# Log-sum-exp over head rows: the middle stage of the tile schedule removed, the half-unit stage begun three tiles earlier

## The chip, the cores and the metric

The kernel runs on one core of a Trainium2 chip. The metric is the device time of one execution in microseconds (us). The text says PE for TensorE, ACT for ScalarE, DVE for VectorE, POOL for GpSimd and SP for SyncE, as the profile does.

## The reference

`x` is 8 x 2048 x 2048 fp32, `bias` is 8 heads x 256 fp32. Each row of 2048 is split into 8 heads of 256 columns; the bias of the head is added, and the log of the sum of the exponentials is taken over the 256 columns. Each result is written twice.

```python
x_heads = x.reshape(B, S, H, Dh).transpose(0, 2, 1, 3) + bias[None, :, None, :]
x_tiled = np.repeat(x_heads, 2, axis=2)
mx = x_tiled.max(axis=-1, keepdims=True)
out = mx.squeeze(-1) + np.log(np.exp(x_tiled - mx).sum(axis=-1))      # 8 x 8 x 4096
```

## The kernel before, in words

The input is read as 64 tiles `t` = 0 to 63 of 256 rows: 128 partitions with `K` = 2 rows each, 2 MB a tile. The kernel sums plain exponentials without subtracting the maximum; a check at the end would redo everything if a sum had run out of range, and does not take place with this data.

Eight tile buffers (`xts`, pairs of them are the four buffers `xb`) hold tiles in turn, so tile `t + 8` is loaded into the buffer of tile `t` once all that read or wrote there have finished. These are gathered in `last_uses[t]`, and `reload(t)` puts the load of tile `t + 8` on SP's queue. Tiles 2 to 41 are loaded in pairs; later ones one at a time, and where a tile is worked in halves (one row of each partition, a "half unit", written 57k0 and 57k1 below) each half has its own load (`load`, `pieces`). A load also waits until the eighth load before it has landed, since there are eight completion semaphores.

There are three ways to the bias. PE can put the bias into PSUM (`put_bias`), add `x` to it with a product with the identity (`add_x`, or `late_heads` in the bulk), and ACT then takes exp from PSUM with its sum at once. POOL can add the bias to `x` in place (`g_add`). Or ACT takes exp of the bare `x`, and exp(bias) is multiplied in later: by a DVE instruction that multiplies and sums one head of one row (`weigh`), or by POOL, which multiplies and halves the columns three times down to 32 (`fold`), after which DVE sums the 32 (`add_fold`).

`STAGES` says which tile is worked how:

- bulk, tiles 0 to 53: PE takes heads 0 to 2, POOL adds the bias of heads 4 to 7, head 3 is multiplied by exp(bias) on DVE (the `mul` in `later`, L430), and one DVE reduction (L437) sums heads 1 to 7.
- mixed, tiles 54 to 56, whole tiles: PE takes head 0, POOL adds the bias of heads 4 to 7 (L412), DVE weighs heads 1 to 3 of both rows (six `weigh`, L453) and one reduction (L437) sums heads 4 to 7.
- half units from tile 57: PE takes heads 0 and 1, one ACT instruction takes exp of the other six (L418), DVE weighs heads 2 to 6, POOL folds head 7. Tiles 62 and 63 vary the shares a little, and tile 63 is loaded in eight pieces.

The order on every engine is the order of the program text, written out by hand: a loop over tiles and their pieces, with two lists of postponed work. `for_pool` holds what follows POOL's step (`later`, `add_fold`, `reload`) and `for_pe` holds ACT's reading of the PSUM sums (`sum_biased`, L393); both are flushed within the next unit, `for_pool` ahead of the unit's own exp, `for_pe` behind it. `keep_warm` puts three dummy products on PE in half units. exp(bias) of heads 1 and 2 is made once in PSUM (`first_factors`: a product that spreads the bias over the partitions, L235, then an ACT exp, L268), in the bank that the bulk uses for head 0. Two tiles after the last one of each of the eight batches, the sums of that batch are transposed on PE (L497) and ACT takes the log (L507). After tile 63 the same is done for the last batch (L606, L612) and the result is stored (L613).

Of the kernel before, what the change touches and what calls it, by code (L numbers as in the profile page):

```python
# [17 lines left out]
K = 2  # L18
# [2 lines left out]

NBUF = 8

NEARLY = 5

NWARM = 3
# [5 lines left out]


BULK = dict(pe=3, acc=1, g0=4, late=True, fold=0)
MIXED = dict(pe=1, acc=1, g0=4, late=False, fold=0)
PROMPT_F1 = dict(pe=2, acc=2, g0=8, late=False, fold=1)
PROMPT_F2 = dict(pe=2, acc=2, g0=8, late=False, fold=2)
SINGLE_F1 = dict(pe=1, acc=1, g0=8, late=False, fold=1)
# [8 lines left out]

STAGES = [
    (0, (BULK,)),
    (54, (MIXED,)),  # L50
    (57, (PROMPT_F1, PROMPT_F1)),
    (62, (SINGLE_F1, SINGLE_F1)),
    (63, (PROMPT_F2, TRIPLE)),
]
# [8 lines left out]
def kernel(  # L63
# [6 lines left out]
    nc = tc.nc  # L70
    P = nc.NUM_PARTITIONS
    B, S, D = x.shape
    H, Dh = bias.shape
# [4 lines left out]
    T = B * NBLK  # L78
    T_PROMPT = STAGES[1][0]
# [36 lines left out]
    xts = [xb[:, k : k + K] for xb in xbs for k in range(0, KB, K)]  # L116
# [8 lines left out]
    def modes_of(t):  # L125
        return [modes for t0, modes in STAGES if t0 <= t][-1]

    def pieces(t):

        if len(modes_of(t)) == 1:  # L130
            return [(0, K, 0, D)]
        cols = [[(0, D)]] * K if t < T - 1 else LAST_COLS
        return [(k, k + 1, c0, c1) for k in range(K) for c0, c1 in cols[k]]

    def rows_of(t, n=1):


        b, at = divmod(t, NBLK)
        if b < B - 1:
            blk, i = divmod(at, TB)  # L140
            v = x[b, blk * P * KB : (blk + 1) * P * KB, :]
            return v.rearrange("(p k) d -> p k d", k=KB)[:, i * K : (i + n) * K]
        v = x[b, at * P * K : (at + 1) * P * K, :]
        return v.rearrange("(k p) d -> p k d", k=K)
# [5 lines left out]
    def on_x(t, ins, after):  # L150
        buf = users[t // TB % len(xbs)]
        for t_u, u in buf:
            same = u.ins.engine == ins.ins.engine
            if u not in after and (not same or t_u % NBUF == t % NBUF and t_u < t):
                tc.declare_no_dep(
                    ins.ins,
                    u.ins,
                    reason="another tile, or waited for by those it waits for",
                )
        buf.append((t, ins))  # L160
        return ins

    loads = {}

    last_uses = [[] for _ in range(T)]

    def load(t):
        if TB <= t < BLOCKS:

            if t % TB == 0:  # L170
                after = [u for i in range(TB) if t >= NBUF for u in last_uses[t + i - NBUF]]
                ins = on_x(
                    t,
                    nc.sync.dma_start(
                        out=xbs[t // TB % len(xbs)], in_=rows_of(t, TB)
                    ),
                    after,
                )
                for i in range(TB):
                    loads[t + i, 0, 0] = ins  # L180
            return
        after = last_uses[t - NBUF] if t >= NBUF else []
        for k0, k1, c0, c1 in pieces(t):
            loads[t, k0, c0] = on_x(
                t,
                nc.sync.dma_start(
                    out=xts[t % NBUF][:, k0:k1, c0:c1],
                    in_=rows_of(t)[:, k0:k1, c0:c1],
                ),
                after,  # L190
            )

    def reload(t):

        n = t + NBUF
        if n < BLOCKS:
            if n % TB == TB - 1:
                load(n - TB + 1)
        elif n < T:
            load(n)  # L200
# [15 lines left out]
    for t in range(NBUF):  # L216
        load(t)
# [16 lines left out]
    def spread(dst, c0, c1):  # L234
        nc.tensor.matmul(  # L235
            dst, lhsT=ones, rhs=brow[:, c0:c1], start=True, stop=True
        )

    for i, c in enumerate(range(G0, D, MM)):
# [11 lines left out]
        out=b_far,  # L251
        in_=brow,
# [5 lines left out]
        out=Rx[0][0:1, 1 + NR :],  # L258
# [7 lines left out]
    def first_factors():  # L266
        spread(one_ps, V0, W0)
        nc.scalar.activation(out=one_ps, in_=one_ps, func=ACT.Exp)  # L268

    def other_factors():  # L270
        nc.scalar.activation(
            out=w_ps[:, W_LATE - W0 :], in_=b_rep[:, W_LATE - G0 : W2 - G0], func=ACT.Exp
        )
        nc.scalar.activation(out=w_sb, in_=b_rep[:, W1 - G0 :], func=ACT.Exp)
# [14 lines left out]
    def put_bias(m, k0, k1):  # L289
# [3 lines left out]
        if m["late"]:  # L293
# [4 lines left out]
            parts = [(ones3, b3)]  # L298
            if n_ps[0] <= NEARLY:
                parts = [(ones3[0:1], bparts[:, i]) for i in range(3)]  # L300
# [164 lines left out]
    def fold(t, k, h0, h1, sums, after):  # L465


        v = xts[t % NBUF][:, k, h0 * Dh : h1 * Dh]
        done = nc.gpsimd.tensor_tensor(  # L469
            out=v, in0=v, in1=w_sb[:, h0 * Dh - W1 : h1 * Dh - W1], op=ALU.mult  # L470
        )
        on_x(t, done, [after])
        v = v.rearrange("p (h j) -> p h j", j=Dh)
        n = Dh
        while n > FOLD:
            n //= 2
            done = nc.gpsimd.tensor_tensor(  # L477
                out=v[:, :, 0:n], in0=v[:, :, 0:n], in1=v[:, :, n : 2 * n], op=ALU.add
            )
            on_x(t, done, [])  # L480

        def add_fold():
            red = nc.vector.tensor_reduce(
                out=sums[:, k, h0:h1],
                in_=v[:, :, 0:FOLD],
                op=ALU.add,
                axis=mybir.AxisListType.X,
            )
            on_x(t, red, [done])

        return add_fold

# [126 lines left out]
    def sums_of(t):  # L619

        b, blk = divmod(t, NBLK)
        if b < B - 1:
            return R[b][:, blk % TB * K :, :, blk // TB]
        return R_last[:, :, blk, :].rearrange("p h k -> p k h")
# [4 lines left out]
    for_pe = []  # L629
# [15 lines left out]
    for t in range(T):  # L645
        if t == T_FACTORS:
            other_factors()
        xt = xts[t % NBUF]
        sums = sums_of(t)
        for k0, k1, c0, c1 in pieces(t):  # L650
            m = modes_of(t)[k0]
            add = None
            heads = []
            if c0 == 0:
                bias_here = bias_there
            if m["late"]:
                pe_part = late_heads(m, t, bias_here, sums)
            else:
                heads = add_x(m, t, k0, c0, c1, bias_here)

                def pe_part(t=t, heads=heads, sums=sums):
                    for k, h, bank, p, mm in heads:
                        sum_biased(t, k, h, bank, p, mm, sums)

            if c0 == 0:
                if next_units and not m["late"]:
                    bias_there = put_bias(*next_units.pop(0))
                if t > T_PROMPT and m["g0"] == H:
                    keep_warm()
                if m["g0"] < H:  # L670
                    add = g_add(m, t, k0, k1)
                if t < T - 1 or k0 == 0:
                    flush(for_pool)
            if t == T_PROMPT and (k0, c0) == (0, 0):
                first_factors()
            h0 = max(c0 // Dh, m["pe"])
            h1 = min(c1 // Dh, m["g0"])
            hf = max(h0, min(h1, H - m["fold"]))
            if h0 < h1 and not m["late"]:
                done = exp_inplace(  # L680
                    t, xt[:, k0:k1, h0 * Dh : h1 * Dh], loads[t, k0, c0]
                )
                if hf < h1:
                    for_pool.append(fold(t, k0, hf, h1, sums, done))
            if c0 == 0:
                flush(for_pe)
            if not m["late"]:
                for k in range(k0, k1):
                    for h in range(h0, hf):
                        weigh(  # L690
                            t,
                            xt[:, k, h * Dh : (h + 1) * Dh],
                            h,
                            sums[:, k, h : h + 1],
                            done,
                        )

            def pool_part(t=t, m=m, k0=k0, k1=k1, sums=sums, add=add):
                if add:
                    later(m, t, k0, k1, sums, add)  # L700
                if k1 == K:
                    reload(t)

            for_pool.append(pool_part)
            if m["g0"] < H:
                pe_part()
                if m["late"]:
                    bias_there = put_bias(*next_units.pop(0))
            elif heads:
                for_pe.append(pe_part)  # L710

        fb, at = divmod(t - 2, NBLK)
        if fb >= 0 and at == NBLK - 1:
            finish(fb)
            ends_of(fb)
            if fb == B - 2:
                store()
# [39 lines left out]
```

## Time and profile before

| | before |
|---|---|
| median of 3 runs (lowest, highest) | 326.43 us (326.16, 326.53) |
| profiled execution, its own time | 327.41 us |
| its span | 325.5 us |
| busy: DVE, POOL, PE, ACT | 289.4, 287.5, 272.7, 265.6 us |
| HBM read, written | 134.23 MB, 1.05 MB |
| mean DMA rate over the span | 416 GB/s |
| granted PE clock, mean | 0.909 |

The span runs from the first to the last instruction of the profiled execution; its own time is 1.9 us more, which lies around the span. Times in the text are us from the start of the span. A busy share is an average over the whole run, and the stages differ; what bounds the end has to be read from the last 60 us.

### The profile page before, as it was taken

The numbers are of one execution on the slowest core, as the hardware profiler recorded it, in microseconds if no ns is written. First come the engines' busy times: TensorE is split into PE (matmuls) and PEld (weight loads), VectorE is DVE, ScalarE is ACT, GpSimd is POOL, SyncE is SP. The second block draws the span as 40 slices with busy tenths as digits, with TensorE's granted clock in tenths as the row PEclk, the third lists the DMA queues.
The fourth block names the chain that finished last, engine by engine and source line by source line (L and its number), as shares of the span: only waits on it lengthen the run. The fifth ranks groups of instructions, "written<-read, shape, count | busy, mean of one in ns | idle before, by whom it ended". The sixth has DMA issues, their size and how long they took to land.

```text
span 325.5 us, 2458 instructions
## 1 busy us (share of the span) xinstructions
PE 272.7 (84%) x695; PEld 102.8 (32%) x695; DVE 289.4 (89%) x329; ACT 265.6 (82%) x426; POOL 287.5 (88%) x120
## 2 busy tenths in 40 slices
PE   5999999878898869888688878698999786598983
PEld 2333333322233323332233323233333232135451
DVE  1346879999999998989989999969999999999996
ACT  1157789898598987889889979869899699989993
POOL 6939997999999899999999999999999999858872
PEclk9977899999597997979899979778999799589999
DMA  8999999999999999999999999999999999999992
GB/s 307 464 403 439 451 417 420 447 439 407 443 443 408 437 435 431 423 439 432 419 443 434 415 443 431 407 433 427 427 421 430 429 424 424 417 421 415 421 391 93
DMA packets 8832, 135.44 MB, mean 416 GB/s; under 512 B 1041, under 2 KB 1425, under 8 KB 2417
## 3 DMA queue, kind: packets, MB, share of 16 engines
q1 hardware_dynamic: 8720, 135.27, 98.0%
q8 instruction: 5, 0.08, 0.1%
q14 instruction: 9, 0.07, 0.1%
q10 hardware_dynamic: 98, 0.01, 0.0%
HBM read 134.23 MB, written 1.05 MB: 416 GB/s over the span
## 4 chain that ended last, share of the span: by engine, by line
DVE 43%; DMA 26%; PE 18%; ACT 8%; POOL 3%; issue 0%; SPq 0%; DVEq 0%
DVE R L437 28%; DMA xb<-in_x_dram 26%; DVE xb L453 9%; PE pair L362 7%; ACT xb L418 6%; DVE xb L430 4%; PE one_ps L362 4%; POOL xb L412 3%; PE pair L303 3%; PE one_ps L303 2%; PE pair L235 1%; ACT xb L380 1%; ACT xb L373 1%; DMA brow<-in_bias_dram 1%; ACT res L507 1%
## 5 line engine op out<-in xcount | busy, mean ns | idle before, releaser
L412 POOL TENSOR_TENSOR xb<-xb,b_rep 128x2048 f32<-128x2048 f32 x57 | 257.3, 4537 | 21.3 <-DMA xb<-in_x_dram 21.1
L437 DVE TENSOR_REDUCE R<-xb 128x14 f32<-128x3584 f32 (+1 forms) x57 | 216.8, 3804 | 1.9
L418 ACT ACTIVATE xb<-xb 128x2560 f32<-128x2560 f32 (+5 forms) x77 | 157.5, 2055 | 8.2 <-POOL xb L412 8.0
L362 PE MATMUL pair<-xb,ident 128*128 128x512 f32 x216 | 117.3, 671 | 0.0
L362 PE MATMUL one_ps<-xb,ident 128*128 128x512 f32 x108 | 68.1, 716 | 10.9 <-DMA xb<-in_x_dram 10.9
L380 ACT ACTIVATE xb<-pair 128x1024 f32<-128x1024 f32 x54 | 56.0, 1038 | 25.0 <-PE pair L362 25.0
L362 PEld LDWEIGHTS pair<-xb,ident 128*128 128x128 f32 x216 | 47.0, 218 | 62.6 <-issue 62.6
L430 DVE TENSOR_TENSOR xb<-xb,w_ps 128x512 f32<-128x512 f32 x54 | 36.8, 681 | 24.0 <-ACT xb L418 23.9
L373 ACT ACTIVATE xb<-one_ps 128x256 f32<-128x256 f32 x108 | 40.4, 387 | 6.7 <-PE one_ps L362 6.7
L303 PEld LDWEIGHTS <-ones 3*128 3x128 bf16 (+1 forms) x192 | 16.8, 95 | 78.0 <-issue 69.0
L303 PE MATMUL one_ps<-b,ones 3*128 3x512 bf16 x49 | 19.1, 390 | 20.9 <-ACT xb L373 20.9
L303 PE MATMUL pair<-b,ones 3*128 3x512 bf16 x98 | 29.1, 376 | 0.0
L362 PEld LDWEIGHTS one_ps<-xb,ident 128*128 128x128 f32 x108 | 17.2, 201 | 33.7 <-DMA xb<-in_x_dram 17.3
L338 PE MATMUL pair<-xb,ident 128*128 128x512 f32 (+1 forms) x36 | 20.5, 656 | 6.3 <-DMA xb<-in_x_dram 6.3
L373 ACT ACTIVATION_READ_ACCUMULATOR xb<-one_ps 128x1 f32 x108 | 23.0, 213 | 0.0
L453 DVE CUSTOM_DVE_ANT_0 xb<-xb,w_ps 128x256 f32<-128x256 f32 x61 | 22.3, 416 | 0.0
L477 POOL TENSOR_TENSOR xb<-xb 128x128 f32<-128x128 f32 (+3 forms) x39 | 13.9, 357 | 3.1
L469 POOL TENSOR_TENSOR xb<-xb,w_sb 128x256 f32<-128x256 f32 (+1 forms) x13 | 10.0, 772 | 5.2 <-ACT xb L418 4.6
L353 PE MATMUL tp<-ident 128*128 128x128 f32 x84 | 13.0, 291 | 0.9 <-ACT res L507 0.9
L507 ACT ACTIVATE res<-tp 32x1024 f32<-32x1024 f32 x7 | 7.1, 1011 | 6.2 <-PE tp L497 6.2
L393 ACT ACTIVATE xb<-pair 128x256 f32<-128x256 f32 x33 | 12.0, 368 | 0.0
L353 PEld LDWEIGHTS tp<-ident 128*128 128x128 f32 x84 | 10.5, 191 | 4.3 <-issue 2.8
(55 smaller groups left out, 91.8 us busy)
## 6 DMA issues: line engine op xcount, KB each, us to landing
xb<-in_x_dram SPq DMA_DIRECT2D x20, 4096.0 KB, 21.3
xb<-in_x_dram SPq DMA_DIRECT2D x17, 2048.0 KB, 22.0
xb<-in_x_dram SPq DMA_DIRECT2D x12, 1024.0 KB, 21.3
xb<-in_x_dram SPq DMA_DIRECT2D x4, 256.0 KB, 13.3
out_dram<-res SPq DMA_DIRECT2D x1, 896.0 KB, 6.8
xb<-in_x_dram SPq DMA_DIRECT2D x2, 384.0 KB, 15.9
xb<-in_x_dram SPq DMA_DIRECT2D x2, 128.0 KB, 6.4
out_dram<-res_last SPq DMA_DIRECT2D x1, 128.0 KB, 1.7
```

The lines of the kernel that those rows point to most:

```text
L303: nc.tensor.matmul(p, lhsT=lhsT, rhs=each_row(b, h * Dh, Dh, K), start=i == 0, stop=False,)
L338: mm = nc.tensor.matmul(p, lhsT=ident, rhs=xts[t % NBUF][:, ka:kb, c : c + w], start=False, stop=True,)
L353: nc.tensor.matmul(tp[:, 0], lhsT=ident, rhs=ident, start=True, stop=True)
L362: mm = nc.tensor.matmul(p, lhsT=ident, rhs=xts[t % NBUF][:, :, h * Dh : (h + 1) * Dh], start=False, stop=True,)
L373: act = nc.scalar.activation(out=xts[t % NBUF][:, k, 0:Dh], in_=got[0][:, k * Dh : (k + 1) * Dh], func=ACT.Exp, accum_out=sums[:, k, 0:1],)
L380: act = nc.scalar.activation(out=xts[t % NBUF][:, :, Dh : m["pe"] * Dh].rearrange("p k (h j) -> p h k j", j=Dh), in_=got[-1].rearrange("p ...
L412: add = nc.gpsimd.tensor_tensor(out=v, in0=v, in1=each_row(b_rep, c - G0, D - c, k1 - k0), op=ALU.add)
L418: return on_x(t, nc.scalar.activation(out=v, in_=v, func=ACT.Exp), [after])
L430: mul = nc.vector.tensor_tensor(out=f, in0=f, in1=each_row(w_ps, m["pe"] * Dh - W0, n, k1 - k0), op=ALU.mult,)
L437: red = nc.vector.tensor_reduce(out=sums[:, k0:k1, h0:H], in_=v.rearrange("p k (h j) -> p k h j", j=Dh), op=ALU.add, axis=mybir.AxisListTy ...
L453: ttr = nc.vector.tensor_tensor_reduce(out=v, in0=v, in1=w, scale=1.0, scalar=0.0, op0=ALU.mult, op1=ALU.add, accum_out=dst,)
L477: done = nc.gpsimd.tensor_tensor(out=v[:, :, 0:n], in0=v[:, :, 0:n], in1=v[:, :, n : 2 * n], op=ALU.add)
```

## The change

The mixed stage is taken out of `STAGES`, and half units begin at tile 54 in place of 57. Tiles 54 and 55 are loaded whole all the same (`WHOLE`), so that both half units of such a tile wait for one load; tile 56 is now loaded in two halves. `first_factors` moves from tile 54 to tile 53, directly behind ACT's reading of that tile's PSUM sums: ahead of tile 53's `later` on ACT. Because tiles 54 and 55 are now half-unit tiles whose buffers are used again (by tiles 62 and 63), `add_fold` counts as a last use, and `reload` for such tiles is put behind ACT's reading of their PSUM sums.

```diff
+WHOLE = (54, 55)
...
-MIXED = dict(pe=1, acc=1, g0=4, late=False, fold=0)
...
 STAGES = [
     (0, (BULK,)),
-    (54, (MIXED,)),
-    (57, (PROMPT_F1, PROMPT_F1)),
+    (54, (PROMPT_F1, PROMPT_F1)),
     (62, (SINGLE_F1, SINGLE_F1)),
     (63, (PROMPT_F2, TRIPLE)),
 ]
...
         after = last_uses[t - NBUF] if t >= NBUF else []
+        if t in WHOLE:
+            ins = on_x(
+                t, nc.sync.dma_start(out=xts[t % NBUF], in_=rows_of(t)), after
+            )
+            for k in range(K):
+                loads[t, k, 0] = ins
+            return
...
-            on_x(t, red, [done])
+            last_uses[t].append(on_x(t, red, [done]))
...
-            if t == T_PROMPT and (k0, c0) == (0, 0):
-                first_factors()
...
-                if k1 == K:
+                if k1 == K and m["g0"] < H:
                     reload(t)
...
             if m["g0"] < H:
                 pe_part()
+                if t == T_PROMPT - 1:
+                    first_factors()
                 if m["late"]:
                     bias_there = put_bias(*next_units.pop(0))
             elif heads:
                 for_pe.append(pe_part)
+            if k1 == K and m["g0"] == H and t + NBUF < T:
+                for_pe.append(lambda t=t: reload(t))
```

`T_PROMPT` is the first tile of the second stage: 54 before and after.

## The prediction

> **What bounds the kernel now.** I read the page's slices first, then the same by stretches at the end, then the timeline of the last 45 us. Times are us from the start of the span.
>
> ```profile
> DVE  1346879999999998989989999969999999999996
> DMA  8999999999999999999999999999999999999992
> DVE 43%; DMA 26%; PE 18%; ACT 8%; POOL 3%; issue 0%; SPq 0%; DVEq 0%
> 278.00:283.00 5.00, 2.64 (x4) 0.63 (x4) 4.96 (x4) 4.56 (x9) 4.56 (x2) 0.50 1.01 421
> 300.00:310.00 10.00, 9.63 (x43) 5.16 (x42) 10.00 (x62) 10.00 (x24) 8.39 (x21) 1.00 1.02 420
> 310.00:320.00 10.00, 7.81 (x39) 4.62 (x38) 10.00 (x62) 9.85 (x29) 7.87 (x16) 1.00 0.94 344
> ```
>
> The slices show the DMA engines full from the second slice on: the input sets the pace. But the chain of waits ends in DVE, and the stretches (busy PE, PE loads, DVE, ACT, POOL, then clock, DMA share, GB/s) show DVE without a gap from 280 to the end. So two clocks run: the loads, and a DVE that trails them. Which one decides is in the timeline:
>
> ```profile
> 278.92 3.89 DVE L437 TENSOR_REDUCE R<-xb 128x14 f32<-128x3584 f32 x1
> 282.72 0.41 DVE L453 CUSTOM_DVE_ANT_0 xb<-xb,one_ps 128x256 f32<-128x256 f32 x1
> ...
> 285.44 1.69 PE L338 MATMUL pair<-xb,ident 128*128 128x512 f32 x2
> ...
> 295.44 0.41 DVE L453 CUSTOM_DVE_ANT_0 xb<-xb,one_ps 128x256 f32<-128x256 f32 x1
> ...
> 312.85 1.70 ACT L418 ACTIVATE xb<-xb 128x1792 f32<-128x1792 f32 x1
> 312.87 0.70 PE L338 MATMUL pair<-xb,ident 128*128 128x256 f32 x2 [0.77 <-DMA xb<-in_x_dram]
> ...
> 315.98 0.41 DVE L453 CUSTOM_DVE_ANT_0 xb<-xb,one_ps 128x256 f32<-128x256 f32 x1
> ...
> 318.12 0.41 DVE L453 CUSTOM_DVE_ANT_0 xb<-xb,w_ps 128x256 f32<-128x256 f32 x1
> ...
> 321.19 0.22 DVE L483 TENSOR_REDUCE R<-xb 128x2 f32<-128x64 f32 x1
> ...
> 321.56 0.30 PE L606 MATMUL tp<-ident,R 128*128 128x128 f32 x1 [2.69 <-DVE R L483]
> ```
>
> Tile 53 leaves DVE at 282.72, when the mixed tiles begin. The first half unit, 57k0, is on PE at 285.44 but on DVE only at 295.44: ten late. Half units land every 2.49 (matmuls released by the DMA at 305.35, 307.84, 310.32) and cost DVE 1.80 (starts 295.44, 297.24), so DVE gains 0.69 a unit and has still not caught up at the end: the exp of 62k1 starts at its landing, 312.85, and is done at 314.55, and DVE takes it up at 315.98. That is 1.43 of pure DVE lateness, and PE's last transposes wait for DVE (2.69). Shorter DVE work anywhere between 282.72 and 315.98 moves the end, up to that 1.43.
>
> **The change, part by part.**
>
> *DVE work of tiles 54 to 56.* Mixed tiles start at 282.72, 286.96, 291.20 and the next stage at 295.44: 4.24 a tile, six weighs of 0.34 and a reduction that holds DVE 2.20. Three take 12.72. Six half units at 1.80 (five weighs of 0.342 and the folded sum, 0.09) take 10.80. DVE is ahead by 1.92 at 57k0. Check by pieces: 12 weighs more, 4.10; three reductions less, 6.60; six folded sums, 0.54: 1.96 less.
>
> [...] The trace has the weigh at 0.342 beside the same PSUM factors.
>
> *POOL.* Three additions of 4.54 go (L412), six folds of 0.73 + 1.19 = 1.92 come: 13.6 against 11.5, one fold per 2.49 of landing. Weighs took 0.34 both beside L412 (283 to 285) and beside folds (from 297), so no price for running together.
>
> *ACT.* A mixed tile costs 1.47 + 0.72 + 1.85 = 4.0 and waits for POOL besides (0.44 and 0.98 at 282.51 and 287.50); a half unit 2.09 (exp starts 293.68, 295.77), 4.18 a tile with no wait for POOL. Worked forward: tile 53's exp ends at 275.9 (next part). From there to the end of 58k0's exp lie nine exps of 1.47, seven PSUM readings of 0.62 and the log of batch 6, 0.95: 294.4, against 295.15 now. At 2.09 a unit against 2.49 of landing ACT meets the loads at 61k1, as now at 62k0. All exps from 62k0 on start at their landings in both kernels.
>
> *The factors.* The spreading product (1.02, L235) now waits for ACT's two readings of tile 53's head 0, which end at 271.80; on PE only the bias for 54k0 queues behind it, which before started at 272.77, behind ACT's L380. On ACT the exp of the factors (0.58, with 0.40 of waiting before) comes ahead of tile 53's big exp, behind which all later ACT work queues. 271.80 + 1.05, and 0.1 to ACT: 273.0, done 273.55; tile 53's exp then ends at 275.9, 0.8 later than now, and exp of 54k0 at 277.4 as now, for the same 0.58 is gone there. The product was not shown here at half clock; bounds are 1.02 and 2.08 (the doubling that L338 shows at 277.93), the second giving 276.9. DVE takes tile 53 at 278.20: hidden by 2.3, at worst by 1.3. If that cover were gone, each us would come off the 1.92.
>
> *Loads.* Tiles 54 and 55 stay one load. Tile 56's load of two becomes two issues of 0.33 on SP with the same rows; loads one per 2.49 or 4.91 leave room, cost nothing. The move of `reload` and the new last use: the load of 62k0 waits for DVE's folded sum of 54k1, about 282.72 + 3.7 = 286.4 (now the reduction's end, 287.04), but it is issued at 290.4 only, when the eighth load before it has landed. Cover 4.0; and 20 us lie between issue and landing, so the DMA engines do not run dry. Landings stay where they are. Without that cover a late load would cost its lateness.
>
> *PE.* Three keep-warm products a unit are added from tile 55 (0.94); a unit then takes PE 2.05 at full clock (296.64 to 298.69), below 2.49. Hidden. At half clock it would not be, which is the slower rival.
>
> *Sum.* The 1.92 is not all paid out. DVE would reach 62k0 at 311.91; its exp ends at 312.07. So DVE starts it at 312.15, and 62k1 at 314.6 instead of 315.98. What is late next is the exp of the landing, and then POOL: the fold of 62k1 ends at 316.63, DVE's weighs of it at 316.65, the folded sum after that lets 63k0 start at about 316.8 instead of 318.12: 1.3. The nine weighs that follow find their exps done (the last, of the piece landing last, at 318.8, needed at 319.5), and the last folded sum finds POOL done (319.6 against 319.9). So the end moves by 1.3. A floor: ACT's last PSUM sum ends at 319.89 and nothing moves it, so the gain cannot pass 1.5. The profiled time would be 327.41 - 1.3 = 326.1; against the median, 0.98 lower, 326.43 - 1.3 = 325.1.
>
> **The rivals.**
>
> *Half the gain or none.* ACT, whose 58k0 I put only 0.75 ahead of now, comes to tile 62 late. PE stood at half clock from about 276.4 to 286.6 in the stage that goes (0.50 in the row above). If it does the same, 55k0, 55k1 and 56k0 start on PE at about 277.9, 282.0, 286.1, and ACT needs 56k0 at 287.4: just met. One half-clock window more (low stretches are 3.41 or multiples in the trace's clock record) delays PE and ACT by 1.7: 62k1's exp ends at 315.3, DVE gains 0.65 or less. 325.8 to 326.4, or 326.1. Against it: PE has more work here than in the mixed stage, and low stretches in the bulk, where PE is 0.8 busy, lasted 3.4 to 6.8.
>
> *Slower.* The same mechanism, two windows more: half clock until 293.4. A unit then takes PE about 4.1 (twice 2.05; by rows between 3.6 and 4.6), against 2.49 of landing; ACT queues in order behind each PSUM sum, and DVE behind ACT. ACT is 3.4 late, gets back 0.40 a unit, and ends 62k1's exp at 317.0, where DVE now takes it up at 315.98: 1.0 worse, 327.4. It decides from one and a half windows past 286.6 on. [...]
>
> *The loads decide.* If DVE's lateness were only the trace's, the end would hang on the last landing and nothing would move: 326.4. Against it stands the 1.43 at 62k1.
>
> **How the numbers follow.** Forecast 0.70; half gain or none 0.12; slower 0.12; loads 0.06. A measurement of this kernel tells some 0.2%, 0.65 us, from no change. So faster 0.70, same 0.18, slower 0.12. Range: from 326.43 - 1.5 less the runs' scatter of 0.3, that is 324.6, to the no-change cases with half that scatter, 326.6; outside it lies mainly the slower case.
>
> **What would show it.** DVE: tile 53 leaves at about 282.7, half units from there 1.80 apart, 57k0 at about 293.5, a wait for ACT (L418's line) at 62k0 or 62k1 where none is now, 62k1 at about 314.6, the last folded sum at about 319.9. ACT: 58k0's exp over at about 294.4. Landings of 62k1 within 0.3 of 312.8. I am wrong if DVE reaches 57k0 later than 294.5, if ACT waits for PE sums (L393's line) between 285 and 300, or if DVE is early and the end does not follow.

## The result, and the profile after

| | before | after |
|---|---|---|
| median of 13 runs (lowest, highest) | 326.26 (325.87, 327.77) | 326.89 us (326.73, 327.45) |
| profiled execution, its span | 327.41, 325.5 | 326.85, 325.1 us |
| granted PE clock, mean | 0.909 | 0.918 |
| DVE instructions on the page | 329 | 356 |
| POOL instructions counted in the trace | 139 | 160 |

The ratio is 1.0022, interval 1.0013 to 1.0031: slower by 0.22%, where 0.4% faster was forecast. The shapes of the two sets of runs differ. Ten of the 13 runs of after lie between 326.73 and 326.96. Those of before scatter, eleven from 325.87 to 326.53 and two above 327.2, and the profiled execution of before (327.41) was such a late one.

The slices and the chain on the page of after, then two stretches (columns as before):

```profile
DVE  1355679999999998999997999999999999999985
DMA  7999999999999999999999999999999999999993
DMA 41%; PE 21%; DVE 20%; ACT 14%; POOL 1%; issue 1%; SPq 0%
```

```profile
278.00:283.00 5.00, 5.00 (x13) 2.27 (x14) 5.00 (x10) 5.00 (x14) 4.45 (x11) 0.66 1.01 421
310.00:320.00 10.00, 8.22 (x38) 4.76 (x38) 8.98 (x52) 9.37 (x24) 7.50 (x16) 1.00 0.93 345
```

The largest share of the chain is no longer DVE's (43% before, 20% now) but that of the loads (41%), and DVE has gaps near the end (8.98 busy of the ten us from 310 to 320, before 10.00). The timeline has the milestones of the forecast:

```profile
277.69 3.89 DVE L444 TENSOR_REDUCE R<-xb 128x14 f32<-128x3584 f32 x1
281.50 0.41 DVE L460 CUSTOM_DVE_ANT_0 xb<-xb,one_ps 128x256 f32<-128x256 f32 x1
...
292.30 0.41 DVE L460 CUSTOM_DVE_ANT_0 xb<-xb,one_ps 128x256 f32<-128x256 f32 x1
...
314.50 0.42 DVE L460 CUSTOM_DVE_ANT_0 xb<-xb,one_ps 128x256 f32<-128x256 f32 x1 [0.27 <-ACT xb L425]
...
320.20 0.22 DVE L490 TENSOR_REDUCE R<-xb 128x2 f32<-128x64 f32 x1
...
320.65 0.33 PE L613 MATMUL tp<-ident,R 128*128 128x128 f32 x1 [1.19 <-ACT xb L400]
...
321.77 0.28 DVE L557 TENSOR_REDUCE verdict<-w_ps 1x1 int32<-1x128 f32 x1 [0.47 <-PE w_ps L556]
```

Tiles 54 to 56 take DVE 10.80 (281.50 to 292.30), as worked out, and 62k1 comes on DVE right behind its exp, with a wait for ACT where DVE was 1.43 late before. Still the execution is only 0.56 shorter than the late one of before, and 0.63 longer by the medians. What the page shows besides: PE's last transposes now wait for ACT (1.19), which before waited for DVE (2.69), and from the start of the verdict reduction to the end of the span pass 325.1 - 321.77 = 3.3, before 2.8.

The DMA view of the stretch from 312 to 316 shows a visitor among the loads (queue, packets, MB, share of the 16 engines). First before, where the loads are alone, then after:

```profile
q1 hardware_dynamic: 820, 1.58, 105.3%
```

```profile
q1 hardware_dynamic: 793, 1.53, 103.4%
q14 instruction: 1, 0.01, 0.5%
```

One packet of 8192 bytes, at 313.27, is program code. By the landing records of the trace (16 for a load, read here as one for each of the 16 DMA engines) one of the 16 is 0.92 to 0.99 behind the others from tile 63's second piece to its last. Tile 62's second half (62k1) landed at 312.75, before 312.83. The second piece of tile 63 landed at 315.35, before 314.48; the last piece at 319.06, before 318.15. In the timeline of after, ACT's first two exps of tile 63 wait for these late pieces:

```profile
315.37 0.84 ACT L425 ACTIVATE xb<-xb 128x768 f32<-128x768 f32 x1 [0.17 <-DMA xb<-in_x_dram]
316.37 0.84 ACT L425 ACTIVATE xb<-xb 128x768 f32<-128x768 f32 x1 [0.15 <-DMA xb<-in_x_dram]
```

### The profile page after: what moved, and what is told of

It is laid out like the page before. It is cut to its first block, busy times and chain, and to the rows that moved or that the text cites. A ratio compares the mean times of both kernels' runs of the same rounds, so it can differ in the third digit from the quotient of the medians.

```text
span 325.1 us, 2588 instructions
## 1 busy us (share of the span) xinstructions
PE 278.4 (86%) x728; PEld 107.1 (33%) x728; DVE 288.2 (89%) x356; ACT 266.9 (82%) x438; POOL 284.3 (87%) x141
## 4 chain that ended last, share of the span: by engine, by line
DMA 41%; PE 21%; DVE 20%; ACT 14%; POOL 1%; issue 1%; SPq 0%
DMA xb<-in_x_dram 41%; DVE R L444 17%; PE pair L369 9%; ACT xb L425 8%; PE one_ps L369 5%; PE pair L310 3%; DVE xb L437 3%; ACT xb L387 2%; PE one_ps L310 2%; ACT xb L380 2%; POOL xb L419 1%; PE pair L242 1%; ACT res L514 1%; PE tp L504 1%; DMA brow<-in_bias_dram 1%
## 5 line engine op out<-in xcount | busy, mean ns | idle before, releaser
L419 POOL TENSOR_TENSOR xb<-xb,b_rep 128x2048 f32<-128x2048 f32 x54 | 243.7, 4536 | 20.3 <-DMA xb<-in_x_dram 20.3
L444 DVE TENSOR_REDUCE R<-xb 128x14 f32<-128x3584 f32 x54 | 209.9, 3888 | 1.9
L369 PE MATMUL pair<-xb,ident 128*128 128x512 f32 x216 | 118.6, 678 | 0.0
L460 DVE CUSTOM_DVE_ANT_0 xb<-xb,w_ps 128x256 f32<-128x256 f32 x79 | 28.5, 416 | 0.1
L345 PE MATMUL pair<-xb,ident 128*128 128x512 f32 (+1 forms) x42 | 21.9, 604 | 4.5 <-DMA xb<-in_x_dram 4.5
L484 POOL TENSOR_TENSOR xb<-xb 128x128 f32<-128x128 f32 (+3 forms) x57 | 20.1, 352 | 4.5
L476 POOL TENSOR_TENSOR xb<-xb,w_sb 128x256 f32<-128x256 f32 (+1 forms) x19 | 14.4, 759 | 8.2 <-ACT xb L425 7.4
L360 PE MATMUL tp<-ident 128*128 128x128 f32 x108 | 17.4, 300 | 0.0
L360 PEld LDWEIGHTS tp<-ident 128*128 128x128 f32 x108 | 14.1, 198 | 4.4 <-issue 3.9
L400 ACT ACTIVATE xb<-pair 128x256 f32<-128x256 f32 x39 | 14.4, 379 | 0.0
```

The lines of the kernel that those rows point to most:

```text
L345: mm = nc.tensor.matmul(p, lhsT=ident, rhs=xts[t % NBUF][:, ka:kb, c : c + w], start=False, stop=True,)
L360: nc.tensor.matmul(tp[:, 0], lhsT=ident, rhs=ident, start=True, stop=True)
L369: mm = nc.tensor.matmul(p, lhsT=ident, rhs=xts[t % NBUF][:, :, h * Dh : (h + 1) * Dh], start=False, stop=True,)
L419: add = nc.gpsimd.tensor_tensor(out=v, in0=v, in1=each_row(b_rep, c - G0, D - c, k1 - k0), op=ALU.add)
L444: red = nc.vector.tensor_reduce(out=sums[:, k0:k1, h0:H], in_=v.rearrange("p k (h j) -> p k h j", j=Dh), op=ALU.add, axis=mybir.AxisListTy ...
L460: ttr = nc.vector.tensor_tensor_reduce(out=v, in0=v, in1=w, scale=1.0, scalar=0.0, op0=ALU.mult, op1=ALU.add, accum_out=dst,)
```

## The experiments

Two lengths describe the end of every profiled execution: from the landing of 62k1 to the start of the verdict reduction, and from there to the end of the span (the tail). The table has the medians of the runs and of the kernel before, run beside them, and the two lengths in the profiled execution. The ratio is taken over the runs as a whole and is not the quotient of the two medians: where runs fall in two groups, as in a_whole, the two can lie on different sides of 1.

| run | median | before | ratio, interval | 62k1 landed | to the verdict | tail |
|---|---|---|---|---|---|---|
| before, profiled (327.41) | | | | 312.83 | 9.83 | 2.8 |
| after, profiled (326.85) | 326.89 | 326.26 | 1.0022 [1.0013, 1.0031] | 312.75 | 9.02 | 3.3 |
| b_again | 325.77 (one run) | 326.05 | | 312.62 | 8.47 | 2.8 |
| b_dve40 | 327.14 | 326.05 | 1.0047 [1.0019, 1.0075] | 313.36 | 9.36 | 2.8 |
| a_warm57 | 326.86 | 326.05 | 1.0017 [1.0005, 1.0029] | 313.00 | 9.01 | 3.3 |
| a_lean | 325.85 | 326.05 | 0.9997 [0.9983, 1.0011] | 312.69 | 8.47 | 2.8 |
| b_lean | 326.01 | 325.96 | 0.9996 [0.9985, 1.0007] | 313.11 | 8.51 | 2.8 |
| b_lean_late | 326.88 | 325.96 | 1.0027 [1.0015, 1.0040] | 313.00 | 9.21 | 2.8 |
| a_lean_late | 325.92 | 325.96 | 1.0002 [0.9988, 1.0015] | 312.90 | 8.47 | 2.8 |
| a_pool5 | 326.10 | 325.96 | 1.0004 [0.9995, 1.0013] | 312.48 | 8.68 | 2.9 |
| a_dve24 | 327.19 | 326.13 | 1.0029 [1.0019, 1.0039] | 312.92 | 8.48 | 3.2 |
| b_pool21 | 326.22 | 326.13 | 1.0008 [0.9997, 1.0020] | 312.51 | 8.58 | 3.2 |
| a_whole | 326.46 | 326.13 | 0.9991 [0.9978, 1.0004] | 312.63 | 9.76 | 2.8 |
| a_whole57 | 325.58 | 326.03 | 0.9985 [0.9976, 0.9994] | 312.28 | 8.47 | 2.8 |
| a_whole_2 | 325.71 | 326.03 | 0.9995 [0.9985, 1.0005] | 312.50 | 9.73 | 2.7 |

The names: b_ is the kernel before with an edit, a_ the kernel after. In the diffs, `...` marks lines left out, and comments behind # are this text's. The theories were these.

1. The 1.43 of DVE lateness belonged to the one profiled execution; the usual run of before has none to give back.
2. Its 27 DVE instructions more move DVE's third code fetch from behind the last landing into the last loads.
3. The tail comes from a sixth code fetch of PE.
4. The tail comes from where POOL's program stands at its end.
5. Formed later: the kernels with the change run in two groups, and the upper one comes from PE's half clock.

**b_again: the kernel before once more.** No edit.

> The kernel before, unchanged, for a second trace. Theory 1 (the DVE lateness that the prediction spent was a property of the one profiled execution, 327.41 us against a median of 326.26): DVE leaves tile 53 near 281.5 instead of 282.72, takes up 62k1 near 314.8 instead of 315.98, and the time is near 326.2. Rival (the lateness is the kernel's): 282.7 and 316.0 again. Both: the last piece of x lands near 318.15, no code fetch of 8 KB falls between 311 and 318, and PE's code is fetched in 16 KB blocks five times, not six.

It took 325.77, 1.64 less than the first profile of the same kernel. DVE's timeline, and PE's last transposes:

```profile
276.97 3.89 DVE L437 TENSOR_REDUCE R<-xb 128x14 f32<-128x3584 f32 x1
...
314.37 0.42 DVE L453 CUSTOM_DVE_ANT_0 xb<-xb,one_ps 128x256 f32<-128x256 f32 x1 [0.23 <-ACT xb L418]
...
319.98 0.30 PE L606 MATMUL tp<-ident,R 128*128 128x128 f32 x1 [1.32 <-DVE R L483]
```

DVE takes tile 53's reduction at 276.97, 1.95 earlier than in the first profile (278.92), and at 62k1 it waits for ACT. There is no lateness to remove in this run. It is one of the fastest of this kernel (the 29 runs beside it have a median of 326.05), so by itself it doesn't tell of the median run; in b_pool21 and b_lean below (8.58 and 8.51 to the verdict) DVE takes up 62k1 0.04 and 0.03 behind the end of its exp, so they show no such lateness either. In the first profile DVE had lost 2.0 between tiles 39 and 40, in the bulk, where the programs are the same, in a half clock of PE that lasted 6.83 from 208 on (3.41 in the profile of after); it stayed late by the same amount to tile 53. The profiles of a_warm57 and a_dve24 have the same stretch and the same loss there. From 62k1's start on DVE is almost without a gap (5.39 busy of the 5.50 from 314.5 to 320), so in this run the 62k1 landing sets the end: 8.47 to the verdict. DVE's third code fetch is there too, but at 319.03, behind the last landing (317.98). The DMA view from 318.5 to 320:

```profile
q1 hardware_dynamic: 59, 0.19, 37.0%
q14 instruction: 1, 0.01, 1.3%
```

The page does not name the engine that a fetch serves. It follows from counting: the third fetch of this kind comes when DVE has issued 316 to 324 instructions by the trace's records (its read-outs and semaphore instructions counted), in every kernel of this study that has one there, whatever the others have issued. In after it comes at 313.27 with DVE's count at 316; b_again reaches that count at 317.90, 4.9 later than after does (313.0), and its fetch comes at 319.03.

**b_dve40: the cost without the change.** The kernel before with

```diff
+    for _ in range(40):
+        nc.vector.memset(pad, 0.0)          # pad is 1 x 1, at the start
```

> The kernel before with 40 tiny DVE memsets (one element each) put early, where DVE has nothing to do. Theory 2 (a DVE code fetch, which is due at a fixed number of DVE instructions, falls into the last loads and holds up one of the 16 DMA engines): the fetch that was at 319.67 comes near 312, the last piece lands near 319.0 instead of 318.15, and the time is 0.4 to 0.8 us above before. Rival (late landings in the kernel after are chance or come from its loads): landings stay at 318.15, the 40 memsets (some 2.5 us early) are hidden, time within 0.2 us of before.

The third fetch moved to 311.28 (DVE's count 316). The DMA view from 310.5 to 312:

```profile
q1 hardware_dynamic: 194, 0.57, 99.2%
q14 instruction: 1, 0.01, 1.4%
```

One DMA engine was set back by 1.0 from 62k1's landing on, and the last piece landed at 318.66. The median is 1.1 above before, with nothing of the change in it, where 0.4 to 0.8 was expected. The profile has a half clock of PE at the end besides (granted clock 0.53 from 314 to 317), so its 9.36 is not the fetch alone. Four of the 12 runs lie at 328.75 to 330.52, which no profile explains, and the interval is wide. So the run shows that the added instructions move the fetch and that the fetch holds up the loads; its price is better read from after and a_lean.

**a_warm57: less PE work in tiles 55 and 56.** The kernel after with

```diff
-                if t > T_PROMPT and m["g0"] == H:
+                if t > T_PROMPT + 2 and m["g0"] == H:
                     keep_warm()
```

> The kernel after with the keep-warm products beginning at tile 57 as before, not at 55: 48 PE instructions less. Theory 3 (a sixth PE code fetch of 16 KB, at 324.0 after the verdict, lengthens the end): no sixth fetch, 2.5 instead of 3.07 us from the start of the verdict's reduction to the end less its own 0.28, time 0.4 to 0.5 below the kernel after, some 0.05% above before. Rival (the products keep PE at full clock and are needed): ACT waits for PE sums between 285 and 300, time as the kernel after or above.

326.86 against 326.89: PE's added work was not the loss. PE fetches code five times here, and the tail is still 3.3, so theory 3 fell; a_lean has the sixth fetch and a tail of 2.8. DVE was 1.15 later here than in the profile of after (tile 53's reduction at 278.84), and 62k1 came at 314.75 with a wait for ACT of 0.27 all the same: with the change, DVE's lateness no longer reaches the end.

**a_lean and b_lean: fewer DVE instructions.** In both, five fills go from DVE to POOL, the two folded sums of a tile become one, and the range check of the bias and of the first seven batches is left out (the sums themselves are all there).

```diff
-    nc.vector.memset(ones, 1.0)
+    nc.gpsimd.memset(ones, 1.0)              # and four more
...
-                out=sums[:, k, h0:h1],
-                in_=v[:, :, 0:FOLD],
+                out=sums[:, k0 : k + 1, h0:h1],   # both rows, in tiles up to 61
+                in_=w[:, :, :, 0:FOLD],
...
-            ends_of(fb)
```

> The kernel after with 29 DVE instructions less ahead of the last loads: five memsets moved to POOL, the folded sums of a tile's two rows (tiles 54 to 61) taken by one reduction instead of two, and the range check left out for the bias and the first seven batches (14 small reductions and 2 more). Theory 2: the DVE code fetch moves from 313.27 to about 318.8, behind the last landing, which comes back to about 318.15 from 319.06; time 0.6 to 0.9 us below the kernel after, that is at or 0.1% below before. Rival (chance, or the loads): the last landing stays near 319.06 and the time stays 0.2% above before.

> The kernel before, with the leaner DVE program of the lean run of after (five fills of constants moved to POOL, the two folded sums of a tile made one in tiles 57 to 61, the range check of the bias and of the first seven batches left out). The third code fetch of DVE lies behind the last landing in the kernel before already, so theory 2 expects nothing from it here: 325.8 to 326.2, last landing about 318.0, tail from the start of the verdict reduction to the end of the span 2.8. If a leaner DVE program was worth about 1 us for another reason (fewer instructions for their own time), this run gains too: 325.0 to 325.3. By theory 1 the slow draws (327 and above) are rarer, because some 0.7 us of DVE work are gone.

In a_lean (29 DVE instructions fewer) the fetch came at 319.42, behind the last landing at 318.04, and no code packet lies between 312 and 319. With five instructions more on POOL, the tail is 2.8 again. The median fell to 325.85, by 1.04 from that of after and by 1.01 from that of a_warm57, which ran beside it. Its DVE and PE rows are those of b_again within 0.1:

```profile
314.44 0.42 DVE L445 CUSTOM_DVE_ANT_0 xb<-xb,one_ps 128x256 f32<-128x256 f32 x1 [0.26 <-ACT xb L410]
...
320.05 0.30 PE L605 MATMUL tp<-ident,R 128*128 128x128 f32 x1 [1.33 <-DVE R L482]
```

The same edit in the kernel before gives nothing (0.9996, with 1 within the interval). So the loss that a_lean wins back is not the time of the instructions left out; they are worth it only where they move the fetch and the tail. And a_lean, which has the whole DVE saving of the change and neither of the two in the way, is only level with before (0.9997): for the runs as a whole there was nothing to gain, which is theory 1.

**b_lean_late and a_lean_late: DVE made late.** Each lean kernel with one more reduction, which holds DVE 1.93, at tile 44 (half of that tile's sums are made twice).

```diff
+        if t == 44:
+            red = nc.vector.tensor_reduce(out=sums[:, 0:1, h0:H], in_=v[:, 0:1]..., op=ALU.add, ...)
```

> The run before it, with one more DVE reduction of 1.95 us (half of tile 44's, made twice) in the middle of the bulk. Theory 1: DVE leaves tile 53 at about 282.3 instead of 280.4 and never catches up, so 62k1 comes on DVE 0.8 to 1.4 after its exp, and the time is 326.8 to 327.4, like the profiled run of the kernel before. Rival (the loads decide in any case, whatever DVE does): no change, 325.8 to 326.2.

> The same added reduction of 1.95 us in the lean kernel after. Theory 1, with the shorter DVE work of tiles 54 to 56 doing what the prediction said: the 1.92 us saved there take up the 1.95 us, DVE waits for ACT at 62k1 as without it, and the time stays at 325.8 to 326.2, some 1 us below the same addition in the lean kernel before. Rival (the change saves nothing on DVE that reaches the end): the same loss as there, 326.8 to 327.4.

Without the change it costs 0.87 (326.88 against 326.01), with it 0.07 (325.92 against 325.85). In both profiles DVE takes tile 53's reduction at 279.15. The row of 62k1 in b_lean_late first, then in a_lean_late:

```profile
315.53 0.40 DVE L446 CUSTOM_DVE_ANT_0 xb<-xb,one_ps 128x256 f32<-128x256 f32 x1
```

```profile
314.65 0.42 DVE L453 CUSTOM_DVE_ANT_0 xb<-xb,one_ps 128x256 f32<-128x256 f32 x1
```

In b_lean_late its exp had ended at 314.74, 0.79 before; in a_lean_late it was taken up at the exp's end. So the step by which 12.72 becomes 10.80 and a late DVE pays it out holds. It needs a late DVE.

**a_pool5 and b_pool21: the tail.** After with five, before with 21 one-element fills on POOL at the start.

```diff
+    for _ in range(5):                        # 21 in b_pool21
+        nc.gpsimd.memset(pad, 0.0)
```

> The kernel after, with five one-element fills on POOL at the start, nothing else. In after the tail from the verdict reduction to the end of the span is 3.3 us instead of 2.8, and POOL stands 0.47 longer over its last eight instructions beside a code fetch at 323.88. Theory 4: POOL's last instructions cross the edge of a code block there, which five instructions more in front move elsewhere; tail 2.8 to 2.9 and 326.3 to 326.5, the last landing still at 319.0 (DVE's program is not touched, so theory 2's part stays). Rival: the tail has to do with the number of DVE instructions or the late landing; then it stays 3.3 and the time 326.8 to 326.9.

> The kernel before with 21 one-element fills on POOL at the start, so that POOL's program has as many instructions as in after (160 against 139), nothing else. Theory 4: POOL meets the edge of a code block within its last instructions here too, the tail is 3.2 to 3.3 instead of 2.8, and the time 326.4 to 326.6, with the landings and the 8.5 from 62k1's landing to the verdict reduction as they were. Rival (the tail comes from the other instructions of after): tail 2.8, 325.9 to 326.1.

The tail went from 3.3 to 2.9 in a_pool5 and from 2.8 to 3.2 in b_pool21. The verdict reduction, first of a_pool5 (span 324.1), then of b_pool21 (span 324.3):

```profile
321.16 0.28 DVE L560 TENSOR_REDUCE verdict<-w_ps 1x1 int32<-1x128 f32 x1 [0.53 <-PE w_ps L559]
```

```profile
321.09 0.28 DVE L553 TENSOR_REDUCE verdict<-w_ps 1x1 int32<-1x128 f32 x1 [0.47 <-PE w_ps L552]
```

In b_pool21, as in after, POOL stands 0.40 between two of its last instructions (323.19 to 323.59) that follow each other by 0.08 in b_again and 0.09 in a_pool5, beside a code fetch at 323.29. The four profiles with 160 POOL instructions (after, a_warm57, a_dve24, b_pool21) all have this gap of 0.4 at the same place and a tail of 3.2 to 3.3; the eleven with 139, 144 or 165 have no such gap and a tail of 2.7 to 2.9. So the tail belongs to the place of POOL's last instructions in its program. How that place decides, the runs don't show. In the program a branch follows the verdict, but no run here shows where its target lies, and none separates it from the edge of a code block, which the expectation of a_pool5 took for the cause.

a_pool5 came out at 326.10, 0.2 to 0.4 below the expectation, and in its profile the other fetch cost less too. It came at 312.91 and set one engine back by 0.95, but by the landing records that engine had been 0.33 ahead of the slowest, so the last landing moved by 0.62 and the way to the verdict by 0.21 (8.68 - 8.47). In after it moved 0.92 and 0.55. In both some 0.4 of the late landing did not reach the verdict. The time of b_pool21 is inconclusive: its interval holds no change as well as the expected 0.4.

**a_dve24: the other half.** After with the merged folded sums and the range check left out as in a_lean, POOL's program as it was.

```diff
-            ends_of(fb)                       # and the merged sums, as in a_lean
```

> The kernel after with 24 DVE instructions fewer and POOL's program as it is (the two folded sums of a tile made one in tiles 54 to 61; the range check of the bias and of the first seven batches is left out). It is the other half of the run with five POOL fills. Theory 2 with theory 4: DVE's third code fetch goes behind the last landing (318.0) and the time from the landing of 62k1 to the verdict reduction falls from 9.02 to 8.5, but the tail stays at 3.3, so 326.3 to 326.5. If the tail belongs to DVE's program, or to the late landing, it falls to 2.8 here and the time to 325.9. If the DVE fetch was worth nothing, the 9.02 stays and the time is 326.8.

The profile is as expected: fetch at 319.17, 8.48 to the verdict, tail 3.2, and 326.36. With a_pool5 and a_lean it makes the two parts separate: DVE's fetch is in the 9.02, POOL's place in the tail. The median is a miss: three runs lie at 326.27 to 326.36, six at 327.02 to 327.63. None of the six was profiled; they may be the upper group of theory 5, and that is not shown.

**a_whole, a_whole_2 and a_whole57: the whole computation again.** To see what the change gives without the fetches, a_whole is after with the five fills on POOL, the merged folded sums, and the range check of the first seven batches made once instead of seven times; it has two DVE instructions more than before. a_whole_2 is the same kernel run again, a_whole57 has the edit of a_warm57 besides.

```diff
-            ends_of(fb)
+            if fb == B - 2:
+                ends_of(fb)                   # over all sums of the seven batches, in one tile
```

> The kernel after with its whole computation, but as many DVE instructions as before has (five fills moved to POOL, the two folded sums of a tile made one in tiles 54 to 61, the range check of the first seven batches made once over all their sums instead of seven times). Theories 2 and 4: neither of the two code fetches is in the way, 8.5 from 62k1's landing to the verdict reduction, tail 2.8, 325.8 to 326.1: the 0.9 us that after lost are back, and nothing more, for the typical run of before waits for the landing of 62k1 and not for DVE. Rival (the shorter DVE work of tiles 54 to 56 is worth something once the fetches are out of the way): 325.0 to 325.4.

> The kernel with its whole computation and as many DVE instructions as before, again, for the profile of another execution. Theory 5: where TensorE's half clock near tile 54 lasts 6.8 us or less, ACT reaches the logarithm of batch 6 at about 292.5, 62k1 is on DVE right behind its exp (8.5 from its landing to the verdict reduction), and the time is 325.3 to 326.0; where it lasts 10.2 us, ACT is 1.5 later and the time 326.5 to 327.1, as in the first profile. Rival: a time of one group with the half clock of the other.

> The kernel with its whole computation and as many DVE instructions as before, with one change: the three keep-warm products (0.94 us of PE) begin at tile 57 instead of tile 55. PE then has 4 x 0.94 us less to do ahead of the transposes of batch 6. Theory 5 (the upper group comes from PE: a half clock of 10 us or more, behind which the transposes and then ACT are 1.5 late): ACT no longer waits for the transposes, the upper group goes or gets rare, and nearly all runs are at 325.3 to 325.6. Rival (the groups come from something else, for example from where a code fetch hits): two groups again, in about the same shares.

The kernel ran in two groups: 325.35 to 325.53 and 326.46 to 327.05 in a_whole, 325.32 to 325.76 and 326.49 to 326.77 in a_whole_2, nine of 19 runs in the upper. Both profiles fell in the upper one. In both PE is at half clock for 10.2 us (274.5 to 284.7, and 274.0 to 284.3), and ACT waits long for the transposes of batch 6 (2.70 and 2.46). In a_whole57 the low stretch is 3.4 long (278.0 to 281.4), as in the profile of after. The stretch from 280 to 283 in a_whole, then in a_whole57 (the third number from the end is the granted clock):

```profile
280.00:283.00 3.00, 3.00 (x9) 1.78 (x9) 3.00 (x14) 3.00 (x10) 2.69 (x7) 0.50 1.03 429
```

```profile
280.00:283.00 3.00, 3.00 (x6) 0.59 (x5) 3.00 (x14) 3.00 (x8) 2.69 (x7) 0.76 1.03 429
```

And ACT's logarithm of batch 6, in a_whole, then in a_whole57:

```profile
294.04 1.01 ACT L530 ACTIVATE res<-tp 32x1024 f32<-32x1024 f32 x1 [2.70 <-PE tp L520]
```

```profile
290.54 1.00 ACT L530 ACTIVATE res<-tp 32x1024 f32<-32x1024 f32 x1
```

In a_whole PE, with keep-warm products in every unit from tile 55 on, was busy without a gap from 277.9 on and came late to the transposes (293.41; 289.62 in a_whole57), ACT in order behind them, and ACT took 62k1's exp at 313.96, 1.33 after its landing: 9.76 to the verdict. Without the products in tiles 55 and 56, ACT does not wait, 62k1 goes straight on, and all 11 runs lie at 325.36 to 326.02: the upper group is gone. a_warm57 agrees: its 12 runs lie at 326.62 to 327.09, where after has three of 13 apart, at 327.34 to 327.45. That PE's late transposes make the upper group is shown by the edit and by the three profiles; that a long half clock starts it is seen in two profiles and was not set by hand, and no run of the lower group of a_whole was profiled.

a_whole57 is 0.9985 of before (0.9976 to 0.9994), the one version whose interval lies below before. Only part of that is understood. It is free of before's late draws and of the upper group; but its usual run, 325.5, is also some 0.4 below the usual run of before, and its profile puts this in the loads, which landed 62k1 at 312.28. Why they were earlier stayed open.

## Why the prediction was wrong

- **DVE work of tiles 54 to 56: right.** 10.80 measured, with weighs 0.34 apart (the single row lasts 0.42 and overlaps the next). DVE came to 57k0 at 292.30, earlier than the 293.5 of the forecast, because it had left tile 53 at 281.50 and not at 282.7; the last of the signs named for being wrong came true: DVE was early and the end did not follow.
- **The sum, the step that failed.** It paid out 1.3 of a lateness of 1.43 that one execution showed, and subtracted that from the median, though that execution stood 0.98 above the median. The same kernel profiled again had no lateness, and waits for ACT at 62k1 (0.23). By that profile, by b_pool21 and b_lean, and by a_lean's being level with before, a usual run had nothing to pay out; the 0.87 of b_lean_late against 0.07 shows what the change is worth where there is something.
- **"Landings stay where they are": wrong, and the first half of the loss.** 62k1 landed as forecast (312.75). But the text gave the added instructions no price beyond their time. They moved a code fetch by some 6 us, into the loads: last landing 0.91 later, 0.55 on the way to the verdict. The floor ("ACT's last PSUM sum ends at 319.89 and nothing moves it") moved with it, to 320.60. A reading of before was off here as well: of the exps from 62k0 on only tile 62's start at their landings; tile 63's first starts at 315.17, 0.69 behind the landing of its piece, behind ACT's own earlier work.
- **The tail: missing from the sum, and the second half.** Six folds in place of three additions, 21 instructions more, brought POOL's last instructions to another place in its program: 0.5 at the very end, where nothing covers it.
- **PE "hidden": wrong in part.** PE took 2.05 a unit as worked out, but at that pace it came late to the transposes, and ACT waited 1.37 for them (292.42), so 58k0's exp was over at 294.81 instead of 294.4. In the profile of after ACT had caught up by 62k1. With 10.2 of half clock (a_whole) it had not, and that cost 1.3. This is the mechanism of the rivals "half the gain or none" and "slower", seen in two profiles, but not the reason for the result. Whether the added products change the length of the low stretch is not shown: it lasted 3.4 in after, and as long in a_warm57 and a_whole57, which leave them out in tiles 55 and 56; a_whole has them and 10.2.
- **POOL: a small miss.** DVE waited 0.2 for a fold three times between 307 and 312, without effect.
- **The rival "the loads decide" was nearest, and got the least weight.** It said that a lateness that was only the trace's would leave nothing to gain; the text set the very row against it that was the trace's. Even it gave no loss.

Put together by the profiles of b_again and after: 62k1 0.13 later, 0.55 for DVE's fetch, 0.5 for POOL's place, 1.2 in all, the difference of the spans (325.1 - 323.9). By the medians the loss is 0.63: the profiled run of after is a usual one (326.85), while b_again is 0.49 below the median of before's 13 runs, and what separates it from them is not shown.

## What to carry to other kernels

Before a stall at the end of one profile is spent, see whether that execution is a usual one: its time against the median is a first sign, and a second profile of the same kernel is the test. An instruction had a place here as well as a duration (DVE's third code fetch came at a count of 316 to 324, and among the last loads it set one DMA engine back by 0.92 to 1.0): where the input stream is full, count how many instructions each engine has issued when its code fetches come, and which of them the edit moves into the last loads or to the end of the program. A gain that a usual run doesn't show can still take up a late one (0.07 against 0.87 here); with DVE leaner by about as many instructions as the change added, and with PE's dummy work kept away from the transposes that ACT waits for, the change became a gain of 0.15%, only part of which is understood.

## What the runs showed of the hardware

- DVE's code came in packets of 8192 bytes, one per about 130 instructions of the trace (counts of 47 to 51, 172 to 189 and 316 to 324), PE's, by the same kind of counting, in packets of 16384 (one per 240 to 274, weight loads counted). One packet among full loads set one of 16 DMA engines back by 0.92 to 1.0 to the end of the stream (after, a_warm57, a_pool5, b_dve40). Each load of `x` has 16 landing records, and the exp that waited for one started behind the last of them (in after at 315.37, landing 315.35). The packet of after took 0.34; why the engine lost more than that is not shown.
- The place of POOL's last instructions made the tail 0.4 to 0.5 longer in four kernels (after, a_warm57, a_dve24, b_pool21), with no change of the work.
- The low-clock stretch of PE that begins between 273 and 280 lasted 10.2 to 17 us in the six profiles without the change (10.2 and 13.7 in the two of the very same program), and 3.4 to 10.2, or was missing (a_lean_late), in the nine with it. One of 6.83 that began at 208, near tile 40, left DVE 1.0 to 1.2 later than in after at tile 45 (before, a_warm57, a_dve24), and the next tiles have no gap in which to catch up. The same length ten us earlier (b_lean, b_dve40, a_pool5) was made up by tile 41.
